# The RWKV projection stage of a two-layer decoder: elementwise work off GpSimd, paired output blocks, and the token-shift weights folded into the low-rank matrices

## The chip, the core and the metric

One core of one Trainium2 chip runs the whole program in one launch. The metric is the device time of that launch in microseconds (us). Engines are named as in the profile: PE is TensorE (matmuls; PEld its weight loads), DVE is VectorE, ACT is ScalarE, POOL is GpSimd, SP is SyncE, which here issues DMAs. L255 is line 255 of the kernel before.

## What is computed

The model has two layers over 2048 tokens of width 1024, all in fp32: layer 0 (retention and stick-breaking attention), layer 1 (RWKV-7 time mixing), each followed by a gated embedding. The change touches the projections of layer 1. Cut to these, the reference is:

```python
xx = token_shift(hn) - hn                    # hn: normalised activations
xs = hn[None] + xx[None] * mu[:, None, None, :]
r, k, v, g = jnp.einsum('pbsd,pdf->pbsf', xs[:4], w_in)
xv, xw, xa = xs[2], xs[4], xs[5]
w_log = -jax.nn.softplus(-(w0 + jnp.tanh(xw @ w1) @ w2)) - 0.5
decay = jnp.exp(-jnp.exp(w_log))
a = jax.nn.sigmoid(a0 + (xa @ a1) @ a2)
kk = (k * k_k).reshape(B, S, H, N)
kk = kk / jnp.maximum(jnp.linalg.norm(kk, axis=-1, keepdims=True), 1e-12)
k = k * (1.0 + (a - 1.0) * k_a)
```

`w_in` holds four 1024x1024 matrices, `w1` and `a1` are 1024x64, `w2` and `a2` 64x1024. A recurrence over tokens then uses r, k, v, kk, a and the decay.

## The kernel before

**Products.** PE works on fp32r operands. `split` (L213) makes two of an fp32 tile: ACT rounds it to `hi` (L215), DVE or POOL subtracts `hi` to give the residual `lo` (L216). `mm3` (L253) then makes one fp32 product of three matmuls, hi·hi (L255), hi·lo (L256) and lo·hi (L257). `weights` (L218) loads a weight, splits it with POOL and stores both parts to DRAM in the first half of the tokens; in the second half it loads the parts (L226).

**The stage.** `l1_proj` (L1052) runs once for each half of 1024 tokens (half 0 and half 1), which it treats as two blocks of 512 tokens (`t`), with 8 blocks of 128 channels (`d` for inputs, `ob` for outputs). `normed` (L1113) makes hn. `mix_half` (L1129) makes one mixed tile xs of 128 channels by 512 tokens: ACT (or, for each third, DVE, L1140) multiplies hn by 1 - mu, DVE adds the shifted hn times mu (L1144), and the split follows with the residual on POOL or DVE. `mix` (L1158) does this for a projection's 16 half-tiles, block after block. `proj_groups` serves r and `run` (L1185) serves k and g by `proj_T` (L259): one output block at a time, its two token blocks in two PSUM banks, the banks of successive blocks alternating. v has its own loop, `proj_N`. `lora` (L1194) mixes xw and xa as well and multiplies them by w1 and a1, 96 matmuls. `k_evac` squares k for the head norms, and after the projection of k a short chain makes their inverses `rn`, split into `rnh` and `rnl`.

**The preparation.** `prep` (L1293) takes 16 steps, one for each output block and token block: six low-rank products (three in rows 0 to 63, three in rows 64 to 127 of PE), two products that spread 1/norm over the channels (`rnp`, L1332 and L1333), tanh and exp on ACT, a scan on DVE, and elementwise products on DVE and POOL (POOL at L1342, L1351, L1357 and L1364), then two stores, ar and kb, on SP's queue.

**What sets the order.** `interleave` weaves generators by weights: r and k with `lora`, one yield each; then v and g with `prep`, 5 yields to 3. The list that this gives is then ordered for each engine by a scheduler at build time, and pools of fixed size let it move work only as far as tiles are free. Weights take their pools in a fixed turn: five buffers of one pool in half 0, and in half 1 a pool of two and a pool of three, in the turn 2, 2, 3, 3, 3. Near the stage's end the loads of the next stage (`stage`, `g`, `o` and its weights) come onto the same queue.

## Time and profile before

| | |
|---|---|
| Time, median of 3 runs | 3871.17 us (3869.03 to 3873.91) |
| The profiled execution | 3869.15 us, its span 3867.3 us |
| Busy: PE, DVE, POOL, ACT | 93%, 54%, 38%, 36% |
| Mean granted TensorE clock | 0.935 of full speed |

Busy time is the time in which an engine had an instruction in work; matmuls overlap in the records, so that a matmul every 0.23 us has a record of 0.39. In a window, PEclk is the granted clock as a share of full speed, and the DMA share is the mean busy share of 16 DMA engines. In lists of instructions a square bracket says how long the engine stood idle before and what ended the wait.

### The profile page before, as it was taken

Reading aid. Unit: us, or ns where it says so; the run is one execution under the profiler, and the core shown is the slowest. Engines: PE = TensorE matmul, PEld = TensorE weight load, DVE = VectorE, ACT = ScalarE, POOL = GpSimd, SP = SyncE. Lnnn points to the kernel's source line nnn. Section 1 sums busy time; section 2 is a strip of 40 time slices with the busy share of each in tenths; the row PEclk is TensorE's granted clock in tenths of the full one; section 3 lists DMA queues with packets and bytes.
Section 4 is the critical chain, followed back from the end, with each engine's and each line's share of the span. In section 5 each row is a group of like instructions: output and inputs, shape, how many; then the busy total and the mean of one; then the engine's idle time right before and its main releaser. Section 6 shows DMA issues by size and latency. Waiting matters only on the chain. (4 is left out here: it accounts for less than half of the span.)

```text
span 3867.3 us, 66663 instructions
## 1 busy us (share of the span) xinstructions
PE 3582.2 (93%) x25961; PEld 2810.7 (73%) x25961; DVE 2100.5 (54%) x3876; ACT 1388.7 (36%) x2705; POOL 1475.7 (38%) x1401
## 2 busy tenths in 40 slices
PE   8999989799989899998879999799999799999978
PEld 6888878676655788787768777576756677777757
DVE  3334542455678333356866656555576566556432
ACT  5233443345442222345532322245433233223233
POOL 4345544554566221456522212243354143222322
PEclk9999999899999999999979999599999889969989
DMA  7258675654566323645446655243467876556485
GB/s 247 86 193 267 207 229 187 208 171 159 180 216 225 137 98 120 185 128 129 90 150 207 191 159 172 79 139 117 151 199 259 220 219 194 164 140 181 154 285 179
DMA packets 560546, 678.82 MB, mean 176 GB/s; under 512 B 179956, under 2 KB 408168, under 8 KB 528744
## 3 DMA queue, kind: packets, MB, share of 16 engines
q1 hardware_dynamic: 476808, 581.62, 47.5%
q10 hardware_dynamic: 42848, 59.39, 4.3%
q0 software_dynamic: 40576, 33.56, 3.8%
q8 instruction: 205, 3.36, 0.4%
q14 instruction: 109, 0.89, 0.1%
HBM read 416.35 MB, written 258.08 MB: 174 GB/s over the span
## 5 line engine op out<-in xcount | busy, mean ns | idle before, releaser
L255 PE MATMUL pj<-act,w 128*128 128x512 f32 x1216 | 499.2, 415 | 28.8 <-ACT act L215 13.3
L256 PE MATMUL pj<-act,w 128*128 128x512 f32 x1216 | 497.9, 410 | 0.8 <-DVE act L216 0.4
L257 PE MATMUL pj<-act,w 128*128 128x512 f32 x1216 | 494.6, 407 | 1.5 <-POOL w L216 1.5
L216 POOL TENSOR_TENSOR w<-wraw,w 128x1024 fp32r<-128x1024 f32 x107 | 247.6, 2320 | 274.5 <-ACT w L215 265.5
L256 PE MATMUL pj<-xs,w 128*128 128x512 f32 x768 | 314.6, 410 | 16.5 <-DVE xs L216 7.9
L255 PE MATMUL pj<-xs,w 128*128 128x512 f32 x768 | 301.3, 409 | 24.1 <-ACT xs L215 22.0
L257 PE MATMUL pj<-xs,w 128*128 128x512 f32 x768 | 308.6, 403 | 0.0
L216 POOL TENSOR_TENSOR xs<-mxa,xs 128x512 fp32r<-128x512 f32 x138 | 202.0, 1480 | 254.3 <-ACT xs L215 244.7
L255 PEld LDWEIGHTS pj<-act,w 128*128 128x128 f32 x1216 | 237.7, 196 | 84.0 <-ACT act L215 18.9
L256 PEld LDWEIGHTS pj<-act,w 128*128 128x128 f32 x1216 | 238.8, 196 | 51.4 <-DVE act L216 2.2
L257 PEld LDWEIGHTS pj<-act,w 128*128 128x128 f32 x1216 | 237.9, 196 | 52.0 <-POOL w L216 2.0
L255 PE MATMUL pj<-w,act 128*128 128x512 f32 x640 | 258.6, 408 | 12.4 <-issue 6.0
L679 DVE TENSOR_TENSOR_SCAN rr<-om,rr,ones 128x512 f32<-128x512 f32 (+3 forms) x160 | 214.9, 1350 | 81.0 <-ACT om L673 72.5
L256 PE MATMUL pj<-w,act 128*128 128x512 f32 x640 | 254.8, 398 | 0.0
L257 PE MATMUL pj<-w,act 128*128 128x512 f32 x640 | 252.0, 398 | 0.0
L688 POOL TENSOR_TENSOR be<-be,rr 128x512 f32<-128x512 f32 (+3 forms) x160 | 167.4, 1049 | 196.2 <-DVE rr L679 89.5
L1144 DVE SCALAR_TENSOR_TENSOR mxa<-hn,vec,mxa 128x512 f32<-128x512 f32 x192 | 183.6, 979 | 41.3 <-ACT mxa L1142 39.1
L255 PEld LDWEIGHTS pj<-xs,w 128*128 128x128 f32 x768 | 146.1, 193 | 82.1 <-ACT xs L215 35.1
L256 PEld LDWEIGHTS pj<-xs,w 128*128 128x128 f32 x768 | 148.7, 194 | 73.8 <-POOL xs L216 20.3
L257 PEld LDWEIGHTS pj<-xs,w 128*128 128x128 f32 x768 | 148.8, 194 | 38.5 <-issue 7.8
L215 ACT CAST xs<-mxa 128x512 fp32r<-128x512 f32 x192 | 114.7, 619 | 126.7 <-DVE mxa L1144 71.0
L215 ACT CAST w<-wraw 128x1024 fp32r<-128x1024 f32 x107 | 106.6, 1001 | 132.4 <-PE pj L257 30.5
(355 smaller groups left out, 8210.1 us busy)
## 6 DMA issues: line engine op xcount, KB each, us to landing
w<-parts SPq DMA_DIRECT2D x147, 1024.0 KB, 6.4
parts<-w SPq DMA_DIRECT2D x99, 1024.0 KB, 5.3
kb<-kb SPq DMA_DIRECT2D x64, 512.0 KB, 4.7
wraw<-in_odd_w_in SPq DMA_DIRECT2D x32, 512.0 KB, 6.1
ar<-ar SPq DMA_DIRECT2D x32, 512.0 KB, 3.6
w<-v SPq DMA_DIRECT2D x128, 128.0 KB, 3.8
xr<-ar SPq DMA_DIRECT2D x64, 256.0 KB, 4.0
kg<-dk POOLq DMA_DIRECT2D x24, 512.0 KB, 5.0
```

Source lines behind the costliest of these rows:

```text
L215: nc.scalar.copy(hi, src)
L216: (lo_eng or nc.vector).tensor_tensor(lo, src, hi.bitcast(F32), op=ALU.subtract)
L255: nc.tensor.matmul(ps, a[0], b[0], start=first, stop=False)
L256: nc.tensor.matmul(ps, a[0], b[1], start=False, stop=False)
L257: nc.tensor.matmul(ps, a[1], b[0], start=False, stop=last)
L679: nc.vector.tensor_tensor_scan(rr[:, 0:kw][:, ::-1], om[:, ::-1], self.ones.to_broadcast([P, kw]), rr[:, kw : kw + 1], op0=ALU.mult, op1=A ...
L688: nc.gpsimd.tensor_tensor(be, be, rr[:, 1 : kw + 1], op=ALU.mult)
L1144: nc.vector.scalar_tensor_tensor(a, hn[d][:, sl], self.col(V_MU + p, d), a, op0=ALU.mult, op1=ALU.add)
```

## The change

In both runs of `l1_proj`:

- Residuals of activations and weights are subtracted on DVE (`lo_eng`), and ACT makes all scalings by 1 - mu. In `prep` POOL's products go to DVE, and `pc` and `kp` go to ACT; `a` is kept as tanh, with its constants folded into `hka`, `oka` and two scalar_tensor_tensors. POOL keeps memsets.
- `proj_pairs` projects r, k and g by two output blocks at a time on all four PSUM banks; the first pair goes token block by token block, as the mixes now come.
- `lora` scales the weights w1 and a1 by 1 - mu and by mu and multiplies them by hn and the shifted hn. The 32 mixes of xw and xa become 16 splits of hn; there are 96 matmuls as before.
- The rows of the 1/norm tile hold hi in 16 rows and lo in the next 16, so that one matmul makes `rnp`. The six low-rank products are written in alternation of their two row halves.
- kb is stored with its two halves in the order of the channels: three DMAs in place of one, two of them in pieces of 64 values.

```diff
-PD = 5
+PD = 3
-    hs = (row == 2 * np.arange(4)[None, :, None] + ch // 64).astype(np.float32)
+    hs = (row % 16 == 2 * np.arange(4)[None, :, None] + ch // 64).astype(np.float32)
...
+    def proj_pairs(self, load, acts, evacs, psp):
+        nxt = [load(0), load(1)]
+        for o0 in range(0, NB, 2):
+            ws = nxt
+            nxt = []
+            pss = [[psp[t].tile([P, TB], F32, tag="proj", name=self.u("pj")) for t in range(NTB)] for _ in range(2)]
+            for ts in [[t] for t in range(NTB)] if o0 == 0 else [range(NTB)]:
+                for d in range(NB):
+                    if len(nxt) < 2 and o0 + 2 < NB and d in (1, 5):
+                        nxt.append(load(o0 + 2 + len(nxt)))
+                    for o in range(2):
+                        for t in ts:
+                            self.mm3(pss[o][t], (ws[o][0][:, d, :], ws[o][1][:, d, :]), acts[d][t], d == 0, d == NB - 1)
+                        if len(ts) > 1 or o:
+                            yield
...
-            def mix_half(p, d, t, x, spread, early=False):
+            def mix_half(p, d, t, x, early=False):
...
-                dve = spread and turn[0] % 3 == 0
-                if dve:
-                    nc.vector.tensor_scalar_mul(a, src, scale)
-                else:
-                    nc.scalar.activation(a, src, AF.Copy, scale=scale)
+                nc.scalar.activation(a, src, AF.Copy, scale=scale)
                 yield
                 nc.vector.scalar_tensor_tensor(a, hn[d][:, sl], self.col(V_MU + p, d), a, op0=ALU.mult, op1=ALU.add)
-                self.split(a, x[0][:, sl], x[1][:, sl], nc.vector if dve else nc.gpsimd)
+                self.split(a, x[0], x[1])
...
+                for t in range(NTB):
+                    for d in range(NB):
...
+                        x = self.act.tile([P, HT], F32R, tag="act", name=self.u("xs"))
+                        xs[d].append((x[:, 0:TB], x[:, TB:HT]))
...
+            self.lo_eng = nc.vector
...
+                    nc.vector.tensor_tensor(sh[:, :, hs], raw[:, :, hs], bc(mu, 4 + j), op=ALU.mult)
+                    nc.vector.tensor_tensor(raw[:, :, hs], raw[:, :, hs], bc(self.omu, 4 + j), op=ALU.mult)
+                self.split(raw, wa[0], wa[1])
+                for q in range(2):
+                    self.split(sh[:, 4 * q : 4 * q + 4], wb[0][q], wb[1][q])
...
+                        x = act2.tile([P, 2, TB + 1], F32R, tag="act", name=self.u("hs"))
+                        self.split(hn[d][:, t * TB : t * TB + TB + 1], x[:, 0], x[:, 1])
...
+                        self.mm3(
+                            pm[t], (wa[0][:, d], wa[1][:, d]), (x[:, 0, 1:], x[:, 1, 1:]), d == 0, False
+                        )
...
+                        for n, (jw, jm) in enumerate(((0, 0), (0, 1), (1, 0))):
+                            for j in range(2):
+                                hs = slice(64 * j, 64 * j + 64)
+                                nc.tensor.matmul(pss[j], w2[jw][hs, oc], mid[jm][hs, sl], start=n == 0, stop=n == 2)
...
-                        nc.tensor.matmul(rnp, x, rnh[hs], start=True, stop=False)
-                        nc.tensor.matmul(rnp, x, rnl[hs], start=False, stop=True)
+                        nc.tensor.matmul(rnp, x, rnc[hs], start=True, stop=True)
...
-                        nc.gpsimd.tensor_copy(self.pc[:, ob, t * NC : (t + 1) * NC], pw[:, :, C])
+                        nc.scalar.copy(self.pc[:, ob, t * NC : (t + 1) * NC], pw[:, :, C])
...
-                        nc.gpsimd.tensor_tensor(kp, kp, k, op=ALU.mult)
+                        nc.vector.tensor_tensor(kp, kp, k, op=ALU.mult)
...
-                        nc.vector.tensor_tensor(a, a, k, op=ALU.mult)
-                        for par in range(2):
-                            hs = slice(64 * par, 64 * par + 64)
-                            nc.vector.tensor_tensor(kb[hs, :, par], cs(a)[hs], cs(en)[hs], op=ALU.mult)
-                            nc.gpsimd.tensor_tensor(kb[hs, :, 1 - par], cs(kp)[hs], cs(en)[hs], op=ALU.mult)
+                        nc.vector.scalar_tensor_tensor(a, a, 1.0, k, op0=ALU.add, op1=ALU.mult)
+                        nc.vector.scalar_tensor_tensor(kb[:, :, 0], cs(a), 0.5, cs(en), op0=ALU.mult, op1=ALU.mult)
+                        nc.vector.tensor_tensor(kb[:, :, 1], cs(kp), cs(en), op=ALU.mult)
                         nc.sync.dma_start(self.d_ar[:, ob, t * NC : (t + 1) * NC], ar)
-                        nc.sync.dma_start(self.d_kb[:, ob, t * NC : (t + 1) * NC], kb)
+                        dkb = self.d_kb[:, ob, t * NC : (t + 1) * NC]
+                        nc.sync.dma_start(dkb[0:64], kb[0:64])
+                        for j in range(2):
+                            nc.sync.dma_start(dkb[64:P, :, 1 - j], kb[64:P, :, j])
```

Three places show how the order of the engines' work moves. The first is DVE at the start of half 0, where hn, the mixes (`mxa`) and their residuals are made. Before:

```order
L1144 SCALAR_TENSOR_TENSOR mxa_1389_6853<-hn_1348_6756,vec_126,mxa_1389_6853 128x512
L1144 SCALAR_TENSOR_TENSOR mxa_1391_6862<-hn_1353_6765,vec_126,mxa_1391_6862 128x512
L1121 SCALAR_TENSOR_TENSOR hn_1358_6777<-hx_1392_6867,vec_126,rb_1342_6740 128x512
L1121 SCALAR_TENSOR_TENSOR hn_1363_6789<-hx_1394_6876,vec_126,rb_1342_6740 128x512
L1125 COPY hnlast_68<-hn_1358_6777 128x1
L1125 COPY hnlast_68<-hn_1363_6789 128x1
L1144 SCALAR_TENSOR_TENSOR mxa_1393_6871<-hn_1358_6777,vec_126,mxa_1393_6871 128x512
L1144 SCALAR_TENSOR_TENSOR mxa_1395_6880<-hn_1363_6789,vec_126,mxa_1395_6880 128x512
```

After (L1154 is the old L1121, L1173 the old L1144, L219 the residual; `hs` is the split hn of the low-rank product):

```order
L219 TENSOR_TENSOR xs_1360_6791<-mxa_1361_6792,xs_1360_6791 128x512
L1154 SCALAR_TENSOR_TENSOR hn_1370_6819<-hx_1371_6820,vec_126,rb_1341_6741 128x512
L219 TENSOR_TENSOR hs_1440_7138<-hn_1362_6797,hs_1440_7138 128x513
L1173 SCALAR_TENSOR_TENSOR mxa_1369_6814<-hn_1366_6808,vec_126,mxa_1369_6814 128x512
L219 TENSOR_TENSOR hs_1444_7178<-hn_1366_6808,hs_1444_7178 128x513
L1154 SCALAR_TENSOR_TENSOR hn_1374_6830<-hx_1375_6831,vec_126,rb_1341_6741 128x512
L219 TENSOR_TENSOR xs_1364_6802<-mxa_1365_6803,xs_1364_6802 128x512
L1173 SCALAR_TENSOR_TENSOR mxa_1373_6825<-hn_1370_6819,vec_126,mxa_1373_6825 128x512
```

The two kinds of residual, which POOL made, now stand between the normalising and the mixing on DVE.

The second is PE in the preparation of half 0, one group of six low-rank products (`lora` tiles, one for each row half of PE). Before:

```order
L255 MATMUL lora_1776_9017<-mid_1345_6753,w_1690_8565 128x512
L256 MATMUL lora_1776_9017<-mid_1346_6754,w_1690_8565 128x512
L257 MATMUL lora_1776_9017<-mid_1345_6753,w_1690_8565 128x512
L255 MATMUL lora_1778_9024<-mid_1345_6753,w_1690_8565 128x512
L256 MATMUL lora_1778_9024<-mid_1346_6754,w_1690_8565 128x512
L1095 MATMUL bnp_1643_8408<-r_1745_8874,hsum_1334_6708 32x512
L257 MATMUL lora_1778_9024<-mid_1345_6753,w_1690_8565 128x512
L1332 MATMUL rnp_1780_9031<-rns_1641_8404,hexp_1336_6712 128x512
```

After:

```order
L1356 MATMUL lora_1729_8869<-mid_1480_7570,w_1646_8431 128x512
L1128 MATMUL bnp_1599_8274<-r_1699_8730,hsum_1334_6710 32x512
L1356 MATMUL lora_1730_8870<-mid_1480_7570,w_1646_8431 128x512
L1356 MATMUL lora_1729_8869<-mid_1481_7571,w_1646_8431 128x512
L1356 MATMUL lora_1730_8870<-mid_1481_7571,w_1646_8431 128x512
L1356 MATMUL lora_1729_8869<-mid_1480_7570,w_1646_8431 128x512
L1356 MATMUL lora_1730_8870<-mid_1480_7570,w_1646_8431 128x512
L1367 MATMUL rnp_1733_8882<-rns_1595_8266,hexp_1336_6714 128x512
```

The two row halves, which came as three and three, alternate, and `rnp` has one matmul. A group like this one is alternated throughout in 13 of 32 cases; 4 are partly so and 15 stand as three and three.

The third is the projection of g in half 1. `w_4688` and `w_4689` are the weights of the first two output blocks before, `w_4582` and `w_4583` after. On PE before:

```order
L256 MATMUL pj_4712_26317<-xs_4665_26127,w_4689_26203 128x512
L257 MATMUL pj_4712_26317<-xs_4664_26126,w_4689_26203 128x512
L255 MATMUL pj_4690_26205<-xs_4668_26138,w_4688_26201 128x512
L255 MATMUL pj_4711_26316<-xs_4668_26138,w_4689_26203 128x512
L256 MATMUL pj_4690_26205<-xs_4669_26139,w_4688_26201 128x512
L257 MATMUL pj_4690_26205<-xs_4668_26138,w_4688_26201 128x512
```

After:

```order
L259 MATMUL pj_4585_25854<-xs_4580_25840,w_4582_25849 128x512
L260 MATMUL pj_4585_25854<-xs_4580_25840,w_4582_25849 128x512
L1367 MATMUL rnp_4601_25948<-rns_4367_24807,hexp_4140_23335 128x512
L1128 MATMUL bnp_4371_24815<-r_4541_25718,hsum_4138_23331 32x512
L1356 MATMUL lora_4617_26054<-mid_4268_24151,w_4410_24952 128x512
L1356 MATMUL lora_4617_26054<-mid_4269_24152,w_4410_24952 128x512
L1356 MATMUL lora_4617_26054<-mid_4268_24151,w_4410_24952 128x512
L258 MATMUL pj_4586_25855<-xs_4550_25753,w_4583_25851 128x512
```

And on SP's queue after, the load of the second block's weight:

```order
L946 DMA stage_4728_26739<-yT_3231_16341 128x512
L949 DMA o_4729_26741<-g_1312_6660 128x512
L946 DMA stage_4730_26746<-yT_3231_16341 128x512
L946 DMA stage_4732_26753<-yT_3231_16341 128x512
L946 DMA stage_4734_26760<-yT_3231_16341 128x512
L229 DMA w_4583_25851<-parts_1833_9366 128x2048
L946 DMA stage_4736_26767<-yT_3231_16341 128x512
L233 DMA wraw_4739_26775<-in_odd_w_out 128x8x128
L1399 DMA kb_4110_23272<-kb_4593_25888 64x8x64
```

Both blocks' products stood interleaved before. Now the second block's weight takes the buffer of the first: its products come after the first's last one, with a few products of the preparation between, and its load stands behind loads of the next stage. The same holds for the seventh block (g6) behind the sixth (g5); before, the third block's load (g2) was the only one to wait in this way.

## Rows read from the trace of the kernel before

**Rows 1.** The page: busy time, share of the span, instructions.

```profile
PE 3582.2 (93%) x25961; PEld 2810.7 (73%) x25961; DVE 2100.5 (54%) x3876; ACT 1388.7 (36%) x2705; POOL 1475.7 (38%) x1401
```

**Rows 2.** Windows, each half's dense work: us; busy PE, PEld, DVE, ACT, POOL; PEclk, DMA, GB/s.

```profile
757.00:1252.00 495.00, 457.73 (x1811) 321.58 (x1811) 346.29 (x348) 217.49 (x343) 278.93 (x196) 0.97 0.56 188
2505.00:2998.00 493.00, 462.99 (x1851) 328.90 (x1847) 293.30 (x351) 201.92 (x331) 204.65 (x172) 0.96 0.51 173
```

**Rows 3.** Windows, stretches of half 0.

```profile
757.00:790.00 33.00, 26.34 (x83) 17.02 (x84) 30.12 (x36) 19.01 (x30) 20.70 (x14) 0.89 0.34 106
790.00:870.00 80.00, 80.00 (x352) 65.65 (x351) 40.64 (x38) 37.06 (x58) 41.19 (x24) 1.00 0.56 183
870.00:920.00 50.00, 41.35 (x154) 28.87 (x153) 37.57 (x40) 31.54 (x52) 30.91 (x19) 0.93 0.27 92
1050.00:1060.00 10.00, 7.33 (x23) 4.43 (x22) 8.33 (x7) 4.84 (x8) 7.74 (x6) 0.83 0.98 357
1110.00:1160.00 50.00, 37.62 (x132) 23.18 (x130) 38.83 (x40) 24.90 (x38) 33.69 (x23) 0.90 0.61 190
1160.00:1250.00 90.00, 84.90 (x326) 55.21 (x325) 78.17 (x80) 25.08 (x42) 55.37 (x45) 1.00 0.63 230
1250.00:1283.00 33.00, 19.82 (x55) 13.77 (x54) 13.02 (x15) 7.26 (x13) 9.75 (x7) 0.69 0.77 268
```

**Rows 4.** Windows, stretches of half 1.

```profile
2510.00:2540.00 30.00, 23.07 (x72) 16.84 (x73) 22.86 (x34) 15.98 (x26) 20.97 (x15) 0.74 0.46 157
2630.00:2670.00 40.00, 33.62 (x132) 23.52 (x131) 33.68 (x36) 23.40 (x39) 21.47 (x14) 1.00 0.23 73
2760.00:2860.00 100.00, 100.00 (x402) 67.77 (x400) 70.81 (x87) 27.47 (x47) 47.20 (x48) 1.00 0.68 215
2860.00:2910.00 50.00, 42.56 (x139) 26.22 (x138) 36.21 (x43) 24.42 (x39) 23.49 (x20) 0.86 0.52 172
```

**Rows 5.** Waits of weight loads, 1110 to 1160 and 870 to 920: us, times, longest.

```profile
PEld pj L255 <- ACT xs L215: 16.0, 11, 6.6
...
PEld pm L256 <- POOL xs L216: 4.8, 4, 2.4
```

**Rows 6.** One line's instructions, DVE mixes and residuals: ns shortest/median/longest, first and last start.

```profile
L1144 DVE SCALAR_TENSOR_TENSOR mxa<-hn,vec,mxa x192: 655/751/2821, 754.1 to 2891.2; 128x512 f32<-128x512 f32 x192
...
L216 DVE TENSOR_TENSOR xs<-mxa,xs x54: 659/693/2447, 797.1 to 2894.2; 128x512 fp32r<-128x512 f32 x54
```

**Rows 7.** Order of time, DVE and POOL between r and k: start us, us, engine.

```profile
879.51 0.69 DVE L216 TENSOR_TENSOR xs<-mxa,xs 128x512 fp32r<-128x512 f32 x1
...
882.51 2.44 DVE L1144 SCALAR_TENSOR_TENSOR mxa<-hn,vec,mxa 128x512 f32<-128x512 f32 x2
...
882.78 6.45 POOL L216 TENSOR_TENSOR xs<-mxa,xs 128x512 fp32r<-128x512 f32 x4 [1.34 <-ACT xs L215]
```

**Rows 8.** Order of time, SP's queue and PE in half 1's projection of g.

```profile
2897.41 0.81 SPq L226 DMA_DIRECT2D w<-parts  x2
...
2902.68 0.77 PE L255 MATMUL pj<-xs,w 128*128 128x512 f32 x1 [1.03 <-DMA w<-parts]
2903.24 0.63 PE L256 MATMUL pj<-xs,w 128*128 128x512 f32 x1
```

**Rows 9.** Order of time, PE in half 0's preparation.

```profile
1171.61 0.39 PE L257 MATMUL lora<-mid,w 64*128 64x512 f32 x1
1171.62 0.49 PE L255 MATMUL lora<-mid,w 64*128 64x512 f32 x1
...
1176.10 0.50 PE L1332 MATMUL rnp<-rns,hexp 32*128 32x512 f32 x1
1176.44 0.39 PE L1333 MATMUL rnp<-rns,hexp 32*128 32x512 f32 x1
```

**Rows 10.** Groups by line, ACT's table loads: us, mean ns, idle time before.

```profile
L918 ACT ACT_TABLE_LOAD x1 | 1.3, 1283 | 2.1 <-DMA g<-g 2.1
```

**Rows 11.** DMA queue, 1010 to 1020 us, v<-ev alone: packets, MB, share of 16 engines.

```profile
q1 hardware_dynamic: 2112, 0.52, 22.2%
```

More of the change, by code (lines that the diff above doesn't have):

```diff
@@ L205, in load_vectors @@
         nc.vector.tensor_scalar(self.omu, v[:, V_MU * NB : (V_MU + 6) * NB], -1.0, 1.0, op0=ALU.mult, op1=ALU.add)
-        self.oka = self.cst.tile([P, NB], F32, name="oka")
-        nc.vector.tensor_scalar(self.oka, v[:, V_KA * NB : (V_KA + 1) * NB], -1.0, 1.0, op0=ALU.mult, op1=ALU.add)
+        self.oka, self.hka = [self.cst.tile([P, NB], F32, name=n) for n in ("oka", "hka")]
+        ka = v[:, V_KA * NB : (V_KA + 1) * NB]
+        nc.vector.tensor_scalar(self.oka, ka, -0.5, 1.0, op0=ALU.mult, op1=ALU.add)
+        nc.vector.tensor_scalar_mul(self.hka, ka, 0.5)
     def col(self, which, b):
@@ L289, in proj_groups @@
                         yield o
+    def proj_pairs(self, load, acts, evacs, psp):
[13 more added lines that the diff above has]
+                            yield
+                if o0 == 0:
+                    for o in range(2):
+                        evacs(o0 + o)(ts[0], pss[o][ts[0]])
+            if o0:
+                for o in range(2):
+                    evac = evacs(o0 + o)
+                    for t in range(NTB):
+                        evac(t, pss[o][t])
+                    yield
     def proj_N(self, ws, acts, evac, psp):
@@ L1183, in to_dram, with load @@
                 return evac
-            def run(p, evacs, xs):
-                wt = self.w_cols(wi[p], 0, f"in1{p}")
-                for ob in range(NB):
-                    nwt = self.w_cols(wi[p], (ob + 1) * P, f"in1{p}") if ob + 1 < NB else None
-                    yield from self.proj_T(wt, xs, evacs(ob), pj)
-                    wt = nwt
-            mid = [sb.tile([P, HT], F32R, tag=f"mid{j}", name=self.u("mid")) for j in range(2)]
+            self.lo_eng = nc.vector
+            def load(p):
+                return lambda ob: self.w_cols(wi[p], ob * P, f"in1{p}")
@@ L1219, in lora @@
+                        q, e = divmod(d, 4)
+                        self.mm3(
+                            pm[t], (wb[0][q][:, e], wb[1][q][:, e]), (x[:, 0, 0:TB], x[:, 1, 0:TB]), False, d == NB - 1
+                        )
                         yield
+                mid.extend(sb.tile([P, HT], F32R, tag=f"mid{j}", name=self.u("mid")) for j in range(2))
                 for t in range(NTB):
@@ L1248, in rk_proj @@
             def rk_proj():
-                load = lambda ob: self.w_cols(wi[0], ob * P, "in10")
-                yield from self.proj_groups(GROUPS_R, load, mix(0, norm=True), lambda ob: to_dram(d_r[ob]), pj)
-                yield from run(1, k_evac, mix(1))
+                yield from self.proj_pairs(load(0), mix(0, norm=True), lambda ob: to_dram(d_r[ob]), pj)
+                yield from self.proj_pairs(load(1), mix(1), k_evac, pj)
             interleave((rk_proj(), 1), (lora(), 1))
@@ L1266, in l1_proj @@
             nc.vector.tensor_scalar_min(rn, rn, 1e12)
-            rnh, rnl = [sb.tile([P, TB], F32R, tag=f"rn{j}", name=self.u("rns")) for j in range(2)]
-            self.split(rn, rnh, rnl)
+            rnc = sb.tile([P, TB], F32R, tag="rn0", name=self.u("rns"))
+            low = self.k[:, C_LOW : C_LOW + 1]
+            sgn = sb.tile([P, 1], F32, tag="sgn", name=self.u("sgn"))
+            nc.vector.tensor_scalar(sgn, low, -2.0, 1.0, op0=ALU.mult, op1=ALU.add)
+            rnh = sb.tile([P, TB], F32R, tag="pw", name=self.u("rnh"))
+            nc.scalar.copy(rnh, rn)
+            rl = ev.tile([P, TB], F32, tag="sg", name=self.u("rl"))
+            nc.vector.tensor_scalar_mul(rl, rn, low)
+            nc.vector.scalar_tensor_tensor(rnc, rnh.bitcast(F32), sgn, rl, op0=ALU.mult, op1=ALU.add)
             def v_proj():
-                xs = mix(2, 0)
+                xs = mix(2)
                 for nh in range(2):
@@ L1288, in g_proj @@
             def g_proj():
-                yield from run(3, lambda ob: to_dram(d_g[ob]), mix(3, 1))
+                yield from self.proj_pairs(load(3), mix(3), lambda ob: to_dram(d_g[ob]), pj)
             bnp = pst.tile([P, TB], F32, tag="pt", name=self.u("bnp"))
@@ L1300, in prep @@
                 late = []
+                pw = sb.tile([P, NC, C + 1], F32, tag="pw", name=self.u("pw"))
+                nc.gpsimd.memset(pw[:, :, 0:1], 1.0)
                 for ob in range(NB):
```

95 lines of the change are left out of this document (39 added, 56 removed).

## The prediction

> **What bounds the kernel now.** I read the busy shares first, then the stage that the change touches by stretches, then the waits of the thin stretches, and last single instructions. The page's first part has TensorE (PE) busy 93% of the span [rows 1]. So a change can win only where PE stands still or runs slowly, or where it does less. The stage runs twice. Its dense work lies between 757 and 1252 us (half 0) and between 2505 and 2998 us (half 1); PE is busy 458 of 495 and 463 of 493 us there [rows 2]. Busy time hides half-speed work, so I count matmuls instead. From 790 to 870 us PE is never idle and starts 352 matmuls in 80 us, 0.227 us each [rows 3]. Where the preparation of the recurrence is woven in, a full stretch starts 402 in 100 us, 0.249 us each, because that work has dearer matmuls [rows 4].
>
> At these prices each stretch shows what it lost, its length less count times price. Half 0 [rows 3]: mixing at the start (757 to 790) 33 - 83 x 0.227 = 14.1 us; from r to k (870 to 920) 50 - 154 x 0.227 = 15.0; 1050 to 1060: 10 - 23 x 0.249 = 4.3; from v to g (1110 to 1160) 50 - 132 x 0.249 = 17.2; 1160 to 1250: 90 - 326 x 0.249 = 8.9; the end (1250 to 1283) 33 - 55 x 0.227 = 20.5. Together 80 us. Half 1 [rows 4]: start 30 - 72 x 0.227 = 13.6; r to k 40 - 132 x 0.227 = 10.0; v to g 50 - 139 x 0.249 = 15.4. Together 39 us. The granted clock falls with the gaps, to 0.69 at the end of half 0 and 0.74 at the start of half 1 [rows 3, 4].
>
> The reader should see what PE lacks there: mixed activations. At v to g PE's weight loads waited 16.0 us for the rounding of xs on ScalarE; at r to k those of the low-rank products waited 4.8 us for POOL itself [rows 5]. VectorE (DVE) is busy 38 of 50 us at r to k [rows 3] although its work is small: an uncontended scalar_tensor_tensor takes 0.66 to 0.75 us and a subtraction 0.69, but both reach over 2.4 us [rows 6]. The reason is in the order of time: with POOL idle the subtraction at 879.5 us takes 0.69 us; two scalar_tensor_tensors at 882.5, beside four POOL subtractions, take 2.44 [rows 7].
>
> **The change, part by part.** *POOL's elementwise work goes to DVE and ScalarE.* With POOL idle I price DVE at the uncontended values of rows 6. One mixed half-tile is then 0.75 + 0.69 = 1.44 us of DVE. Preparing one (channel block, half) is a scan and eight other operations, some 1.2 + 8 x 0.72 = 7 us. A weight's residual is twice 0.69 = 1.4 us, thirty-three times, in half 0 alone. Half 0 then gives DVE 64 x 1.44 + 16 x 1.44 (normalising, and the residual of hn for the low-rank product) + 33 x 1.4 + 16 x 7 = 273 us against 346 now [rows 2]. That fits beside some 420 us of PE work, so DVE is no bound.
>
> *Mixing starts earlier.* In a pair the last two output blocks pass over the channels together, so the first tiles come free some 22 us before the projection ends (96 matmuls x 0.227) instead of 11. Sixteen mixes at 1.44 us need 23 us, and the next pair's first half uses them up only at six matmuls (1.4 us) per channel. I give back nearly all of r to k (13 of 15.0; 9 of 10.0) and v to g (15 of 17.2). At 1050 the weight's residual was late: 4 of 4.3. In 1160 to 1250 DVE is busy 78 of 90 us [rows 3] and becomes loose: 7 of 8.9. At the end of half 0 the next layer's activations wait for tiles of the same pool and for the last preparation; both come sooner: 12 of 20.5. At the start DVE still has per half-tile hn, mix, residual and residual of hn, 4 x 0.72 = 2.9 us, while PE has 12 matmuls, 2.7 us; the low-rank products fill PE there, but DVE remains level with it: 6 of 14.1 and 4 of 13.6. Half 0 gets 57 us, half 1 13 plus v to g, taken next.
>
> *Weight buffers in half 1.* Pools there hold two and three weights in fixed turn. w2 of the preparation now falls into the pool of two and stays until the end, so of the pair (g0, g1) both need the one buffer left: in the order the load of g1 and its matmuls stand right behind g0's last, and the same happens between g5 and g6. Before, g2 waited so: its load was issued at 2897.4 us and the matmul began at 2902.7; the matmuls behind it took 0.63 us in the record [rows 8], against 0.39 at full clock [rows 9]. With about 2 us of other products in that gap and some 13 slow matmuls at 0.2 us more, such a wait costs about 6 us. One goes, which I leave in the 15.4 of v to g (14 back); two come. Bounds 5 (as before) to 12 (eleven 256 KB loads now stand ahead of g1's on SP's queue, whose wait also holds stores of kb behind it). I take 7.5, nearest the measured one: +15.
>
> *Fewer and closer products.* One of two rnp products goes: the second begins 0.34 us after the first [rows 9], 32 times: -11. The six low-rank products of the preparation may alternate between rows 0 to 63 and 64 to 127. Where the halves meet today, the matmuls begin 0.01 us apart, not 0.23 [rows 9]. In the order 13 of 32 groups alternate throughout (two more such meetings, 0.46 us), 4 partly, 15 not at all: -7. The low-rank products of the projection stay 96 per half; their 32 mixes become 16 splits, already counted on DVE.
>
> *What is added.* A pair takes all four PSUM banks, so the next pair waits for copies that had a whole block's time before. The order staggers the ends and puts head sums or low-rank products between; 18 borders at 0 to 2 us (two copies in a row), and I take 0.4, near nothing since fillers stand there: +7. Four more activation-table loads of 1.28 us [rows 10] fall at the end of half 1, where gates of the next stage mix with Exp and Tanh: 0 to 5, I take +2. ScalarE's three added operations per preparation step lie under PE work (ScalarE is busy 25 of 90 us there [rows 3]); without that cover they would cost 16 x 2 us per half, at DVE's 0.7 each. Each kb store becomes three DMAs, two of them in 256-byte pieces: 1024 pieces. In 1010 to 1020 us 2112 packets of that kind took 22.2% of 160 engine-microseconds, 17 ns each [rows 11], so a step adds 1.1 us of all engines at most, since the large packets that they replace go. At 63 to 68% DMA share [rows 3, 4] that is hidden: 0; were DMA full, 2 x 16 x 1.1 = 35 us.
>
> The Trainium skill speaks against those pieces: "DMA: Bandwidth & Descriptors" says in its opening table that line rate needs at least 512 bytes and that below it the DMA reads, modifies and writes. If that doubled a piece's price and nothing were hidden, the sum would be 70 us worse. The trace has pieces of the same size at 17 ns each, as they move [rows 11], so I keep the sum.
>
> *Sum.* -57 (half 0) - 27 (half 1: 4 + 9 + 14) - 11 - 7 + 15 + 7 + 2 = -78 us. Other stages keep their work; the recurrences are only reordered a little by the scheduler, which I put at 0 within 10. The profiled execution took 3869.15 us (span 3867.3), so 3791; the median of the runs is 2 us higher, and I give **3792 us**.
>
> **The rivals.** *More (chance 0.15), 3760.* The weight waits are filled (5 each instead of 7.5), the end of half 0 closes wholly and the starts too: 5 + 8 + 17 = 30 more. For it: today's thin stretches all hang on the same lack. Against it: DVE is level with PE at the starts.
>
> *Half 1 gives nothing (0.2), 3822.* The two weight waits take 12 each and the blocked queue holds the preparation up, so what half 1 won (27) less its waits is gone: 9 for the waits, and 20 for bank borders at 1.5 us instead of 0.4. For it: the order shows both waits with hardly any filler. Against it: the wait seen in rows 8 was short.
>
> *The pieces fill the DMA (0.02), 3827.* The preparation then waits for its stores in both halves, 35 us as worked out above. For it: 98% DMA share at 1050 [rows 3]. Against it: 63 to 68% in the long stretches.
>
> *DVE becomes the bound (0.06), 3930, slower.* If DVE's long durations do not come from POOL but from the stage's traffic, it carries POOL's work at about 1.0 us per operation. Half 0 then has some 400 operations, 400 us against 346, half 1 334 against 293 [rows 2]; that is 95 us more on an engine that already sets the pace where PE is thin, of which I put two thirds (63) on the path. The point is 0.85 us per operation: above it the bursts at the borders outlast PE's cover. Against it: rows 7, and the medians of rows 6.
>
> *It doesn't do what it says (0.05), 3870.* The order alternates only 13 groups, and the mixes could still wait for tiles, so gaps move and gains meet new waits. Against it: DVE's relief in all stretches.
>
> **How the numbers follow.** The forecast has 0.49, with 3775 to 3808 as its own range; 0.03 lies between 3845 and 3863. Below 3863 (0.2%, 7.7 us, about what a measurement tells from no change) lie 0.49 + 0.15 + 0.2 + 0.02 + 0.03 = 0.89: faster. Same 0.05, slower 0.06. The range 3745 to 3840 takes the forecast, most of the more and of the half-1 case, and leaves out about 0.2.
>
> **What would show it.** Right: in the stage POOL has nothing but small memsets and no DVE operation of 128x512 but the scan stands above 0.8 us; the thin stretches at r to k and v to g are full; PE pairs of low-rank products begin within 0.02 us; half 1 has two holes of 4 to 8 us, before g1 and before g6, with a half clock behind each. Wrong: a mean mix above 0.85 us on DVE, PE waiting for xs at the borders as before, waits for PSUM copies above 1 us at most of the 18 borders, or DMA share near 1.0 in the preparation.

## The result, and the profile after

The changed kernel takes **3779.12 us** (median of 4 runs, 3773.11 to 3787.24) against 3871.52 before: a ratio of 0.9759, 95% interval 0.9744 to 0.9773. It is faster by 92 us; the forecast was 3792 (3745 to 3840), from a sum of -78.

The page's first part, which answers to [rows 1]:

```profile
PE 3536.1 (93%) x25929; PEld 2801.1 (74%) x25929; DVE 1954.3 (52%) x3884; ACT 1412.1 (37%) x2767; POOL 986.2 (26%) x1036
```

POOL lost 490 us of work, and DVE, which took most of that over, has 146 us less. The groups of instructions of DVE in half 0 show why. The first three are before, the next three after, the last column of numbers ahead of the second bar being the mean in ns:

```profile
L1144 DVE SCALAR_TENSOR_TENSOR mxa<-hn,vec,mxa 128x512 f32<-128x512 f32 x96 | 97.1, 1034 | 17.5 <-ACT mxa L1142 16.2
...
L1140 DVE TENSOR_SCALAR mxa<-hn,omu 128x512 f32<-128x512 f32 x27 | 31.3, 1158 | 32.7 <-POOL xs L216 32.7
...
L1352 DVE SCALAR_TENSOR_TENSOR k<-k,vec,rnp 128x512 f32<-128x512 f32 x16 | 11.7, 731 | 10.7 <-POOL kp L1351 10.7
```

```profile
L1173 DVE SCALAR_TENSOR_TENSOR mxa<-hn,vec,mxa 128x512 f32<-128x512 f32 x64 | 46.9, 748 | 1.5 <-ACT mxa L1171 0.9
L219 DVE TENSOR_TENSOR xs<-mxa,xs 128x512 fp32r<-128x512 f32 x64 | 43.4, 686 | 15.9 <-ACT xs L218 15.6
...
L1384 DVE SCALAR_TENSOR_TENSOR k<-k,vec,rnp 128x512 f32<-128x512 f32 x16 | 11.9, 745 | 1.1 <-PE rnp L1367 0.3
```

The same mix takes 748 ns where it took 1034. The product by `rnp`, one of whose inputs lies in PSUM, took 731 ns beside a busy POOL and takes 745 now: it was never slowed.

Windows of the stretches that answer to [rows 3] (the start of half 0, r to k, v to g, its end) and to [rows 4] (start, r to k, v to g, g6); columns as there:

```profile
766.50:799.50 33.00, 33.00 (x135) 26.38 (x134) 30.19 (x54) 21.44 (x36) 0.00 (x0) 0.94 0.38 128
845.00:895.00 50.00, 49.72 (x219) 40.69 (x218) 27.91 (x40) 32.60 (x55) 0.00 (x0) 1.00 0.52 174
...
1080.00:1130.00 50.00, 48.07 (x193) 34.25 (x191) 41.20 (x58) 34.59 (x55) 0.00 (x0) 0.97 0.81 258
...
1200.00:1233.00 33.00, 28.73 (x113) 20.26 (x112) 13.97 (x21) 11.14 (x21) 5.98 (x4) 0.90 0.87 319
2465.00:2495.00 30.00, 29.89 (x126) 23.33 (x126) 28.28 (x54) 24.84 (x39) 3.16 (x2) 0.97 0.37 131
2550.00:2590.00 40.00, 39.85 (x174) 32.31 (x173) 23.29 (x36) 27.73 (x48) 0.00 (x0) 1.00 0.40 140
...
2790.00:2830.00 40.00, 29.31 (x76) 16.17 (x76) 32.65 (x49) 30.59 (x48) 0.00 (x0) 0.74 0.74 255
2890.00:2910.00 20.00, 13.53 (x45) 9.28 (x44) 12.64 (x18) 8.08 (x17) 0.00 (x0) 0.74 0.71 231
```

At the prediction's prices of a matmul the losses are now 2.4 us (before 14.1), 0.3 (15.0), 1.9 (17.2) and 7.3 (20.5) in half 0, and 1.4 (13.6) and 0.5 (10.0) in half 1. Only the last two rows are worse than before: 21.1 and 8.8 us. There the products of g1 and of g6 stand behind the last of g0 and of g5. What PE waited for between 2790 and 2910 us (in total, times, longest):

```profile
PE pj L258 <- DMA w<-parts: 6.5, 1, 6.5
PE lora L1356 <- ACT sg L1359: 4.2, 1, 4.2
PE pj L259 <- DVE xs L219: 3.3, 6, 1.8
PE pj L258 <- ACT xs L218: 3.2, 5, 1.0
```

The first of the two places in order of time, SP's queue and PE:

```profile
2816.15 0.32 SPq L229 DMA_DIRECT2D w<-parts  x1
```

```profile
2815.79 1.92 PE L1128 MATMUL bnp<-r,hsum 128*32 128x512 f32 x2
2821.87 1.65 PE L1356 MATMUL lora<-mid,w 64*128 64x512 f32 x3 [4.16 <-ACT sg L1359]
2823.44 0.80 PE L258 MATMUL pj<-xs,w 128*128 128x512 f32 x1
2824.04 0.63 PE L259 MATMUL pj<-xs,w 128*128 128x512 f32 x1
```

The load of g1 is issued at 2816.2 us, when g0 has ended; g1's matmuls begin at 2823.4, at the slow clock (0.63 us). The 4.16 us in brackets are put down to ScalarE, which is late for `sg` of the preparation, so they are not the weight's own wait. Ahead of them g0, alone, waited 6.5 us for mixes. At g6 the wait of 6.5 us is the weight's.

To place the gain I use two lines whose first and last starts mark the stage: the normalising (hn) and the copies at the end of the preparation (bon). Their rows after:

```profile
L1154 DVE SCALAR_TENSOR_TENSOR hn<-hx,vec,rb x32: 740/749/1539, 762.1 to 2461.0; 128x512 f32<-128x512 f32 x32
```

```profile
L1415 DVE COPY bon<-btp x8: 180/181/192, 1221.1 to 2928.2; 128x32 f32<-128x32 f32 x8
```

Half 0 is then 1221.1 - 762.1 = 459.0 us, half 1 2928.2 - 2461.0 = 467.2. The same for every profile (g 0 and g 1 run from the same hn to the start of the last product of g in that half; part A runs from the first hn to the last, part B from there to the end of the span):

| profile | half 0 | g 0 | half 1 | g 1 | part A | part B |
|---|---|---|---|---|---|---|
| before | 507.8 | 506.9 | 488.9 | 479.4 | 1758.3 | 1356.5 |
| after | 459.0 | 446.0 | 467.2 | 466.0 | 1698.9 | 1324.5 |
| after, again | 459.2 | 447.3 | 466.5 | 465.4 | 1705.7 | 1325.4 |
| e1_w2_out | 459.6 | 445.3 | 449.7 | 440.2 | 1690.6 | 1317.1 |
| e2_res_pool | 484.2 | 470.8 | 493.4 | 492.2 | 1737.4 | 1359.1 |
| e3_prep_pool | 447.1 | 443.1 | 469.5 | 468.3 | 1692.7 | 1342.3 |
| e4_no_pair | 444.4 | 440.1 | 445.0 | 433.4 | 1699.8 | 1324.0 |
| e5_rnp4 | 455.1 | 452.4 | 473.4 | 472.3 | 1720.0 | 1336.3 |
| e6_lora33 | 458.4 | 446.1 | 465.4 | 464.2 | 1697.0 | 1318.9 |
| e7_kb_one | 464.3 | 444.4 | 467.6 | 466.5 | 1689.3 | 1336.2 |
| e8_before_res_dve | 474.1 | 459.3 | 469.3 | 454.7 | 1692.3 | 1328.4 |
| e9_pool_aside | 508.6 | 495.2 | 509.4 | 508.2 | 1761.8 | 1369.7 |
| e10_pa4 | 459.5 | 466.8 | 464.5 | 465.0 | 1707.8 | 1348.2 |
| e11_pool_out | 476.5 | 462.6 | 467.2 | 448.2 | 1701.8 | 1328.9 |

The lengths need care. Up to 33 matmuls of the next stage, about 8 us, lie inside some of them (22 in half 0 of the changed kernel, 33 in e7_kb_one, none there before, in e3_prep_pool and in e4_no_pair), and in half 0 of e10_pa4 g ends behind the preparation. What lies outside the two halves varies too. Between them (from bon of half 0 to the last hn of half 1) the profiles took from 1218.2 us (e8_before_res_dve, granted clock 0.94) to 1264.9 (e5_rnp4, 0.92), behind half 1 from 853.5 (e6_lora33, 0.91) to 883.7 (e10_pa4, 0.89). Why the clock differs there is not shown.

Part A won 59 us and part B 32, 22 of these in half 1. In the profiled run what PE does ahead of the stage, in the same order, took 9.6 us longer (762.1 against 752.5). The two profiles of the changed kernel differ by 6.8 us in part A, so differences of that size are not read as effects.

### The profile page after: what moved, and what is told of

Same layout as the page of the kernel before. It is cut to its first block, busy times and chain, and to the rows that moved or that the text cites. A ratio compares the mean times of both kernels' runs of the same rounds, so it can differ in the third digit from the quotient of the medians.

```text
span 3785.5 us, 66193 instructions
## 1 busy us (share of the span) xinstructions
PE 3536.1 (93%) x25929; PEld 2801.1 (74%) x25929; DVE 1954.3 (52%) x3884; ACT 1412.1 (37%) x2767; POOL 986.2 (26%) x1036
## 4 chain that ended last, share of the span: by engine, by line
PE 32%; DMA 8%; DVE 7%; SPq 3%; ACT 1%; issue 1%; POOL 1%; ACTq 0%; POOLq 0%; DVEq 0%
PE pj L258 6%; PE pj L259 6%; PE pj L260 6%; PE g L1490 2%; PE y L1652 2%; PE s L1630 1%; PE y L1649 1%; DMA wraw<-in_odd_w_out 1%; DMA w<-parts 1%; PE u L1593 1%; DMA g<-g 1%; DVE prd L1521 1%; PE x L1615 1%; PE kt L1603 1%; DVE wb L1527 1%
## 5 line engine op out<-in xcount | busy, mean ns | idle before, releaser
L258 PE MATMUL pj<-xs,w 128*128 128x512 f32 x768 | 298.4, 403 | 18.1 <-DMA w<-parts 6.5
L259 PE MATMUL pj<-xs,w 128*128 128x512 f32 x768 | 307.0, 400 | 5.2 <-DVE xs L219 5.1
L260 PE MATMUL pj<-xs,w 128*128 128x512 f32 x768 | 302.4, 397 | 0.0
L258 PEld LDWEIGHTS pj<-act,w 128*128 128x128 f32 x1216 | 237.8, 196 | 72.0 <-ACT act L218 11.3
L219 POOL TENSOR_TENSOR w<-wraw,w 128x1024 fp32r<-128x1024 f32 x72 | 159.4, 2218 | 173.4 <-ACT w L218 152.1
L1490 PE MATMUL g<-xr,kb 64*128 64x128 f32 x1024 | 149.7, 309 | 34.9 <-DVE grb L1498 20.6
L1490 PEld LDWEIGHTS g<-xr,kb 64*128 64x128 f32 x1024 | 121.6, 203 | 60.0 <-DVE grb L1498 22.2
L258 PEld LDWEIGHTS pj<-w,act 128*128 128x128 f32 x640 | 121.9, 191 | 39.2 <-ACT sg L535 10.3
```

The source lines that it names most:

```text
L219: (lo_eng or nc.vector).tensor_tensor(lo, src, hi.bitcast(F32), op=ALU.subtract)
L258: nc.tensor.matmul(ps, a[0], b[0], start=first, stop=False)
L259: nc.tensor.matmul(ps, a[0], b[1], start=False, stop=False)
L260: nc.tensor.matmul(ps, a[1], b[0], start=False, stop=last)
L1490: nc.tensor.matmul(ps[:, j], kb[br, 4 * g + j], xr[br, par, 4 * g + j], start=True, stop=True)
```

## The experiments

Times are medians; runs named together in one heading ran beside each other.

**The changed kernel again, and e1_w2_out.**

> The changed kernel once more, beside the others. Every theory: 3779 us within 8, since its four runs so far lie between 3773 and 3787.

It took 3784.53 us (0.9777, 0.9759 to 0.9796).

```diff
 # in prep, behind the load of w2
+                if w:
+                    self.wps = self.wps[:-1]
```

> In half 1 the pool that w2 holds a buffer of gets no further turn behind it, so g1 and g6 are loaded ahead as the others are. Theory (the two weight waits, with the slow clock behind them, are the holes in the projection of g): the trace of the changed kernel has 77 matmuls in the 40 us from 2790 and 45 in the 20 us from 2890, which at 0.249 us leaves 20.8 and 8.8 us; about 5 of the first are the border from v to g, so 20 to 25 us go and the time is 3755 to 3760. Rival (the holes are mixes that come late at the border, the weights would only have come in their shadow): no more than 9 us, 3770 or above.

Measured: 3772.28 us (0.9751, 0.9726 to 0.9776), 12 us less than the kernel beside it, with overlapping intervals. In its profile the stretch from v to g is full:

```profile
2773.00:2813.00 40.00, 40.00 (x172) 29.91 (x170) 32.90 (x49) 29.88 (x49) 0.00 (x0) 1.00 0.77 270
```

172 matmuls in 40 us, where there were 76. So the fixed turn made the hole, and the rival falls: with the turn mended the mixes come in time, and PE had waited for them only while g0 ran alone. The last product of g comes 25 us sooner (440.2 against 465.4) and half 1 is 17 us shorter (449.7 against 466.5). But the time misses the theory's 3755 to 3760, and part B is only 8 us shorter: half of the 17 is given back behind the stage, which takes 867.4 us at a mean granted clock of 0.88, against 858.9 at 0.90 beside it. Why the clock is lower is open.

**e2_res_pool and e3_prep_pool**, in the same row of runs.

```diff
-                self.split(a, x[0], x[1])
+                self.split(a, x[0], x[1], nc.gpsimd)
...
-            self.lo_eng = nc.vector
+            self.lo_eng = nc.gpsimd
...
```

> The changed kernel with the residuals of activations and weights back on POOL in this stage; the preparation stays on DVE and ACT. Theory (POOL beside DVE makes both slow, and that starved PE at the borders): the mixes of DVE, 0.75 us now, go to 0.9 us or more in the mean, r to k and v to g thin out again, and the time is 25 to 50 us longer, 3804 to 3829. Rival (the earlier mixing by pairs closed the borders, whoever subtracts): the mixes may be slower, but the time stays within 8 us of 3779.

Measured: 3847.53 us (0.9938, 0.992 to 0.9955), 63 us longer than the changed kernel beside it: more than the theory's range. The mixes of half 0:

```profile
L1173 DVE SCALAR_TENSOR_TENSOR mxa<-hn,vec,mxa 128x512 f32<-128x512 f32 x64 | 90.6, 1440 | 149.6 <-ACT mxa L1171 149.6
```

1440 ns instead of 748. The rival, that pairs close the borders whoever subtracts, falls by the time, but not wholly by the borders. The start of half 0, r to k and v to g:

```profile
758.00:791.00 33.00, 25.68 (x88) 17.79 (x87) 27.44 (x23) 16.08 (x27) 29.43 (x19) 0.87 0.41 127
860.00:910.00 50.00, 46.84 (x199) 38.13 (x198) 27.59 (x18) 30.90 (x51) 32.73 (x20) 0.97 0.43 143
1090.00:1140.00 50.00, 42.94 (x164) 29.73 (x164) 28.30 (x27) 31.71 (x52) 30.05 (x19) 0.93 0.69 205
```

At the same prices these lose 13.0, 4.8 and 9.2 us, where the kernel before lost 14.1, 15.0 and 17.2. So with slow mixes the rest of the change still closes two thirds of r to k and half of v to g.

```diff
-                        nc.vector.tensor_tensor(kp, kp, k, op=ALU.mult)
+                        nc.gpsimd.tensor_tensor(kp, kp, k, op=ALU.mult)
...
```

> The changed kernel with four operations of each preparation step back on POOL (kp times k, ar of r, the copy pc, the second half of kb). Theory (the same contention, but mostly under PE's work): DVE's operations of the preparation go from 0.69 to about 1 us, and the time is 5 to 20 us longer, 3784 to 3799. Rival (all of POOL's part in the preparation lay off the path): within 4 us of 3779.

Measured: 3800.31 us (0.9818, 0.9798 to 0.9838), 16 us longer, as the theory has it. DVE's operations are slower too: `a` times k takes 1311 ns in half 0 instead of 685, ar of k 962 instead of 685. But by the table half 0 is not longer for it (447.1, g 0 443.1) and part B is 17 us longer, so where those 16 us arise is not settled.

**e4_no_pair, e5_rnp4, e6_lora33 and e7_kb_one.** The first gives k and g a loop of one output block in two banks:

```diff
-                yield from self.proj_pairs(load(1), mix(1), k_evac, pj)
+                yield from self.proj_one(load(1), mix(1), k_evac, pj)
...
```

> The kernel of e1_w2_out with k and g projected one output block at a time, both token blocks together, as before the change (r stays paired). Theory (the pairs set the mixing early enough, and the first pair goes token block by token block as the mixes come): the borders r to k, k to v and v to g thin out by 5 to 10 us each where they touch k or g, in both halves, 15 to 40 us in all: 3787 to 3812 against 3772. Rival (with POOL idle the mixes are quick enough by themselves): within 8 us of 3772.

Measured: 3792.21 us (0.9791, 0.9757 to 0.9824), 20 above e1_w2_out, which ran in another row with an overlapping interval. In the table both halves are shorter than with pairs (444.4 and 445.0). Neither the preparation nor the last product of g is later for it in the stage (g 0 is 440.1 and g 1 433.4, with pairs 445.3 and 440.2), so the theory falls there, as far as pairs of k and g go. What the kernel loses, it loses elsewhere: the stretch between the halves in e1_w2_out, then in e4_no_pair:

```profile
1214.20:2445.20 1231.00, 1153.82 (x10506) 944.37 (x10504) 694.95 (x1498) 409.35 (x916) 398.81 (x498) 0.93 0.50 142
1201.60:2457.00 1255.40, 1172.54 (x10525) 959.30 (x10525) 688.51 (x1501) 412.00 (x920) 402.95 (x501) 0.91 0.49 142
```

It takes 24 us longer for 19 more matmuls, at a lower granted clock, and the stretch behind half 1 takes 12 us longer (879.0 against 867.4). Whether that hangs on the pairs is not shown.

```diff
-                        nc.tensor.matmul(rnp, x, rnc[hs], start=True, stop=True)
+                        for _ in range(4):
+                            nc.tensor.matmul(rnp, x, rnc[hs], start=True, stop=True)
```

> The changed kernel with the product rnp made four times over instead of once (32 x 3 more matmuls in the preparation). Theory (PE is the bound there, each costs the 0.34 us by which the second followed the first): 32 x 3 x 0.34 = 33 us longer, 3812 to 3818. Rival (the preparation has slack on PE, so the product that was saved was worth little): under 12 us, at most 3795.

Measured: 3817.36 us (0.9842, 0.9814 to 0.9871), 33 to 38 us above the changed kernel's two medians, as the theory has it. The price of one is smaller in the trace:

```profile
1012.75 1.20 PE L1368 MATMUL rnp<-rns,hexp 32*128 32x512 f32 x4
1013.88 0.50 PE L259 MATMUL pj<-w,xs 128*128 128x512 f32 x1
```

Four hold the array for 1.13 us, and one in the changed kernel for 0.43 (next fence), so each more costs 0.23 us, and 96 of them would make 22 us of the 33. In the stage less than that shows: the last product of g comes 5 and 7 us later (452.4 and 472.3, beside 447.3 and 465.4), 12 in all, which is as much as the rival allows. The stretch between the halves is 18 to 25 us longer than in the changed kernel's two profiles (1264.9 against 1246.5 and 1239.9). So the time is the theory's, but that PE is the bound all through the preparation is not shown.

```diff
-                        for n, (jw, jm) in enumerate(((0, 0), (0, 1), (1, 0))):
-                            for j in range(2):
+                        for j in range(2):
+                            for n, (jw, jm) in enumerate(((0, 0), (0, 1), (1, 0))):
```

> The changed kernel with the six low-rank products of a preparation step written as three and three again; in the order 31 of 32 groups then stand so, 13 to 17 groups less alternate. Theory (alternating row halves lie beside each other on PE): 5 to 8 us longer, and in the trace the groups of three and three take about 0.46 us more than alternated ones. Rival (the scheduler mixes other products in anyway, so nothing is saved): within 3 us.

Measured: 3779.95 us (0.9747, 0.9721 to 0.9772), the time of the changed kernel. The order of time on PE shows groups of six in the kernel before (three and three), after (alternated) and in e6_lora33 (three and three):

```profile
1026.68 0.51 PE L255 MATMUL lora<-mid,w 64*128 64x512 f32 x2
1027.02 0.40 PE L256 MATMUL lora<-mid,w 64*128 64x512 f32 x2
1027.26 0.40 PE L257 MATMUL lora<-mid,w 64*128 64x512 f32 x2
1027.59 0.50 PE L256 MATMUL pj<-w,xs 128*128 128x512 f32 x1
```

```profile
1027.53 0.97 PE L1356 MATMUL lora<-mid,w 64*128 64x512 f32 x6
1028.42 0.49 PE L1367 MATMUL rnp<-rns,hexp 32*128 32x512 f32 x1
1028.85 0.50 PE L258 MATMUL pj<-w,xs 128*128 128x512 f32 x1
```

```profile
1023.07 0.97 PE L1356 MATMUL lora<-mid,w 64*128 64x512 f32 x6
1023.97 0.49 PE L1367 MATMUL rnp<-rns,hexp 32*128 32x512 f32 x1
```

All three hold PE for 0.90 us: the two row halves already ran side by side. In the kernel before that holds for 12 of the 16 groups of half 0; in the other four the second half starts only behind the first.

```diff
-                        nc.sync.dma_start(dkb[0:64], kb[0:64])
-                        for j in range(2):
-                            nc.sync.dma_start(dkb[64:P, :, 1 - j], kb[64:P, :, j])
+                        nc.sync.dma_start(dkb, kb)
```

(kb is then made in its two row halves on DVE.)

> The changed kernel with kb made in its two row halves again (four DVE operations on 64 rows instead of two on 128) and stored by one DMA in large pieces. Theory (the 256-byte pieces are hidden beside PE's work, and DVE has room in the preparation): within 4 us of the changed kernel, 3779 to 3785. Rival (the pieces fill the DMA queue in front of the loads): 10 to 35 us faster than it.

Measured: 3782.77 us (0.9761, 0.9735 to 0.9787), as the theory has it. The DMA queue's row of the changed kernel, then of this one:

```profile
q1 hardware_dynamic: 510056, 577.95, 49.3%
```

```profile
q1 hardware_dynamic: 478312, 577.95, 49.1%
```

31,744 packets more took 0.2% more of the engines' time.

**e8_before_res_dve, e9_pool_aside and e10_pa4.** The first is one part alone, in the kernel before:

```diff
-                self.split(a, x[0][:, sl], x[1][:, sl], nc.vector if dve else nc.gpsimd)
+                self.split(a, x[0][:, sl], x[1][:, sl], nc.vector)
...
-            self.split(raw, w[:, 0], w[:, 1], nc.gpsimd)
+            self.split(raw, w[:, 0], w[:, 1], self.lo_eng)
...
```

> The kernel before with one part of the change alone: the residuals of activations and weights of this stage on DVE, POOL's part in the preparation left. Theory (POOL beside DVE was the cost of the borders): 25 to 60 us faster than before, 3812 to 3847 against 3872. Rival (only together with fewer mixes and the pairs does DVE have room): within 10 us of before.

Measured: **3784.1 us** (0.9754, 0.9729 to 0.9779). This is more than the theory's range and all of the change's gain. The start of half 0, r to k and v to g:

```profile
761.00:794.00 33.00, 27.10 (x106) 19.47 (x106) 32.14 (x58) 21.83 (x35) 0.00 (x0) 0.97 0.37 113
865.00:915.00 50.00, 48.51 (x203) 36.03 (x202) 37.74 (x59) 34.70 (x57) 0.00 (x0) 1.00 0.45 144
1080.00:1140.00 60.00, 54.51 (x209) 35.67 (x208) 54.13 (x72) 31.04 (x47) 12.43 (x12) 0.94 0.73 245
```

They lose 8.9, 3.9 and 8.0 us, with the whole change 2.4, 0.3 and 1.9. The difference, 16 us, is about the 15 by which half 0 is longer here (474.1 against 459.0).

```diff
+                for _ in range(2):
+                    nc.gpsimd.tensor_tensor(scr, x, x, op=ALU.mult)
```

> The changed kernel with POOL given work that nobody waits for: behind each of the 128 mixed half-tiles it squares the residual twice (448 columns) into a scratch tile. PE's order is that of the changed kernel, row for row. Theory (POOL's mere running beside DVE makes DVE slow): DVE's mixes go from 0.75 to 1 us or more in the mean, and the time is 20 to 60 us longer, 3800 to 3840. Rival (in e2_res_pool PE waited for POOL's own late residuals): the mixes stay at 0.75 us and the time within 8 us of 3780.

Measured: 3878.77 us (1.0001, 0.9985 to 1.0016): the whole gain is gone, by work whose result nobody reads. DVE's mixes of half 0, its product by `rnp`, and POOL's added work:

```profile
L1180 DVE SCALAR_TENSOR_TENSOR mxa<-hn,vec,mxa 128x512 f32<-128x512 f32 x64 | 78.0, 1237 | 0.2 <-ACT mxa L1178 0.2
...
L1392 DVE SCALAR_TENSOR_TENSOR k<-k,vec,rnp 128x512 f32<-128x512 f32 x16 | 11.9, 745 | 0.8
```

```profile
L1165 POOL TENSOR_TENSOR scr<-xs 128x448 f32<-128x448 f32 x128 | 165.9, 1296 | 264.9 <-DVE xs L219 251.4 <-DVE hnlast L1158 5.3
```

PE's order is the changed kernel's, so the rival, POOL's own lateness, falls: its mere running makes DVE slow. ScalarE is not slowed (its scalings take 723 ns, in the changed kernel 721). The squares read the residual's tile and could have kept it from being used again, but no wait in the trace ends with one of them.

```diff
-PA = 5
+PA = 4
```

> The kernel of e1_w2_out with the weave of v and g with the preparation at 4 to 3 yields instead of 5 to 3. Theory (the preparation comes last at the end of both halves, where the trace of the changed kernel has 53 and 45 matmuls in 20 us, and 8 us are lost each): 5 to 12 us faster than e1_w2_out, 3760 to 3767. Rival (DVE and ACT then come late for the mixes of g, and the end is only moved): within 5 us of 3772 or slower.

Measured: 3826.0 us (0.986, 0.9829 to 0.9891), 54 us above e1_w2_out. The theory falls, and the trace shows most of the loss: the last product of g comes 21 us later than in e1_w2_out in half 0 (466.8 against 445.3) and 25 us later in half 1 (465.0 against 440.2). PE waits for the preparation, in half 1 by this wait above all (in total, times, longest):

```profile
PE rnp L1369 <- DVE k L1386: 14.6, 3, 6.3
```

In half 0 the same wait is 11.3 us, and e1_w2_out has it in neither half. So the preparation, drawn ahead, came too soon for DVE, whose product reads the `rnp` before; in the longest case (8.7 us in half 0) DVE in its turn waited for the load of k. The rival is right that it is slower, but the mixes of g are not the main wait.

**e11_pool_out.** The kernel before with POOL emptied in this stage (as in e8_before_res_dve, and `kp`, ar, `pc` and kb on DVE and ACT) and the turn of e1_w2_out.

> The kernel before with POOL taken out alone: the residuals on DVE as in e8_before_res_dve, POOL's four operations of a preparation step on DVE and ACT, and the pool that holds w2 left out of the turn in half 1 as in e1_w2_out; no pairs, no folded low-rank weights, no merged rnp, kb in one store. Against e1_w2_out (3772 us), which has all of these as well. Theory (the other parts pay as the single runs say: pairs 20, rnp 11): about 31 us longer than it, 3795 to 3810. Rival (with POOL out, the rest of the change is worth nothing in all: e8_before_res_dve was at 3784, the preparation's part was worth 16 in e3_prep_pool): 3755 to 3775.

Measured: 3796.94 us (0.9796, 0.9777 to 0.9815), 25 above e1_w2_out, which was in another row of runs. The rival falls: with POOL out and the turn mended, the rest of the change (pairs, folded weights, one `rnp`) is worth 17 us in each half by the table (by the last product of g 17 and 8) and 25 in the time. Since the pairs of k and g show nothing there (e4_no_pair), the folded weights, `rnp`, the pairs of r and the scalings that go from DVE to ACT are left; none of these was tested alone but `rnp`. DVE has 343 us of work in half 0 here (760 to 1230 us) against 255 in the changed kernel (765 to 1215 us). Against e8_before_res_dve both halves are the same within 3 us, so emptying POOL's part of the preparation alone brought nothing to half 0, nor, together with the mended turn, to half 1; the 13 us between their times lie outside the stage and are open.

## Why the prediction was right, and where it was not

**POOL and DVE: right, and larger than put.** The mean of a mix was priced at 0.75 us and is 748 ns; DVE's work of half 0 was put at 273 us and is 255 (765 to 1215 us). The rival in which DVE becomes the bound is out. The Trainium skill has the mechanism in "SBUF — State Buffer", section "Who interferes with whom": a DVE instruction with two SBUF inputs contends with a POOL instruction that reads SBUF, one with a single SBUF input does not, unless it runs in a mode that uses both of DVE's ports. The trace agrees: the mix went from 1034 to 748 ns, and the product by `rnp` stayed (731, 745). The `tensor_scalar` of the mixing has one input and yet took 1158 ns beside POOL, against 486 in e8_before_res_dve. The Trainium skill names that form, in the same section, among those that can run in such a mode.

**"Mixing starts earlier": the gain was right, its cause only in part.** r to k and v to g in half 0 gave back 14.7 and 15.3 us (put at 13 and 15), the starts more than put: 11.7 and 12.2 instead of 6 and 4. I ascribed the borders to the pairs, which begin the mixing some 22 us ahead. e8_before_res_dve, without pairs but with DVE at its own speed, gives back 11.1 and 9.2 of the two borders, and e2_res_pool, with the rest of the change but slow mixes, 10.2 and 8.0. So either closes most of r to k and about half of v to g; with both, 30.0 of the 32.2 us that the two borders had lost came back. Pairs of k and g alone show none of it (e4_no_pair); r stayed paired in every run that has the rest of the change. At the start DVE's speed gave 5.2 of the 11.7, about the 6 that were put; the rest came with the other parts. The folded weights, which leave DVE 16 residuals in place of 32 mixes with theirs, are the likely one, but were not tested alone. What the rest of the change won beyond e8_before_res_dve, 15 us in half 0 (474.1 to 459.0), was gone again by the start of half 1 (part A 1692.3 against 1698.9): the stretch between the halves took 1218.2 us there, at a granted clock of 0.94, and 1239.9 in the changed kernel, at 0.93. Why is open. In half 1 the weight waits took it.

**The weight buffers: the place was right, the term too small for the projection.** Two holes, before g1 and g6, stand where they were put, with the slow clock behind them, though the first has only 0.7 us of the weight's own wait after the 4.16 of `sg`. +15 was the term. Less the 1.4 that [rows 4]'s 15.4 was to keep, the two windows lose 29.9 - 1.4 = 28.5 us. With the turn mended (e1_w2_out) g ends 25 us sooner, the preparation 17 and the kernel 12. So the projection paid nearly twice the term, the preparation and the time about the term. The price came from one old wait [rows 8], ahead of which two blocks had run side by side. Here g0 ran alone ahead of g1 and used up the mixes twice as fast.

**Fewer and closer products.** -11 for `rnp`: 0.23 us each by e5_rnp4's trace is 7.4, by its time 11 to 13, by the last product of g in its stage 4. -7 for alternation was wrong: I read 0.23 us between matmuls into 0.90 us groups that already overlapped; the group of [rows 9], where the second half starts late, is one of the four exceptions.

**What is added.** kb's pieces cost nothing that shows in the time, as put (e7_kb_one). The Trainium skill puts the least transfer for line rate at 512 bytes ("DMA: Bandwidth & Descriptors", section "Specifications"). The estimate of 70 us that the prediction made of it is not borne out by any run. The bank borders were put at 7 us; in the waits of the stage PE waited 3.6 us in half 0 and 1.5 in half 1 for copies and squares of finished banks. The table loads were not tested alone.

**The sum.** -57 and -27 were put for the gaps; the windows listed give back 11.7 + 14.7 + 15.3 + 13.2 = 55 in half 0 (of 46 put for these four), and in half 1 12.2 + 9.5 at the first two (13 put) against the larger holes. The mis-sized terms offset each other. By the table the two halves are 48.8 and 21.7 us shorter, 70.5 of the 78 that were put. Outside them the profiled runs differ by 9.6 us lost ahead of the stage, some 10 won between the halves and some 10 behind half 1 (32 in part B, of which 22 in the stage), which I had put at 0 within 10 without a term. So that the time came within 13 us of the forecast is in part luck.
